# Two first-layer heads of a hybrid decoder trunk: output rows turned by transposing transfers, and taken over before and behind the next head's scores

## The chip, the cores and the metric

The kernel runs on one core of a Trainium2 chip. The metric is the device time of one execution in microseconds. A run of the kernel before gives 984.02 us as the median of three (984.0 to 984.71). The engines are TensorE (PE in the profile; its weight loads PEld), VectorE (DVE), ScalarE (ACT), GpSimd (POOL) and SyncE (SP), which issues most transfers; ScalarE issues some too.

## The reference

528 tokens (16 learned ones and 512 of input) of 1024 channels go through two layers, a gated linear attention with four heads of 512 output channels, and a differential softmax attention with eight; then comes a norm. The change lies in the first layer:

```python
proj = xn @ w_in
q, k, v, z, g_lr = jnp.split(proj, ...)
...
_, o_real = lax.scan(gla_chunk, S1, (chunks(q), chunks(k), chunks(v), chunks(lg)))
...
o = head_rms(o.transpose(0, 2, 1, 3)).reshape(B, L, D_INNER) * gnorm
y = jax.nn.silu(z) * o
return y @ w_out
```

`head_rms` normalizes the 512 channels of a token in one head. All of it is computed in float32.

## The kernel before

**Number format.** A float32 operand of TensorE is held as two rounded halves, hi and lo (`split`: a copy on ScalarE that makes hi, then a subtraction on VectorE that makes lo), and a product is three passes, hi*hi, hi*lo, lo*hi. So every weight tile gives a row such as wh<-raw on ScalarE and one such as wl<-raw on VectorE before TensorE can use it. Most projections are done in a scheme with sums of weight blocks (rows wl<-sum, a11h, a12h and the like), whose results land in the PSUM tiles bx, by, bv and are put together on ScalarE and VectorE as t, u, ks and so on.

**Layouts.** Projections come out with channels on partitions and tokens along the row. The state products of a head come out the other way, tokens on partitions. The output product needs channels on partitions again, so the outputs have to be turned.

**A head.** The loop over `hd` = 0 to 3 runs, for each head: the gate z; its scores (`gla_scores`, then `gla_cross` for blocks 1 to 4 through `gla_ready`); then `gla_blocks` over five blocks of tokens (block 0 has the 16 learned tokens, blocks 1 to 4 have 128 each). For a block, `output(b)` makes the products in a PSUM tile `po`, squares and sums them on ScalarE, takes the root on GpSimd, and scales `po` on ScalarE into the tile `on`, whose tag is t. `rows(b)` turns `on` by four TensorE transposes into a PSUM tile (L1258), multiplies by z on VectorE (L1260) and splits the product into y (L269 on ScalarE, L270 on VectorE). The output product of head `hd`, `q_gla_out`, reads y in the next head's iteration: for heads 0 and 1 behind the next head's v units, for head 2 among the blocks of head 3.

**The order of work on TensorE.** It is written by hand. A `Weaver` W holds a queue of generators of projection work. `W.fill(us)` takes from this queue for so many microseconds of estimated TensorE time, and is called between the steps of a head, so that TensorE has projections to do while the other engines finish a step. During the blocks of head `hd` the filling is the q and k units of head `hd`+1. `W.follow(...)` starts steps after so much woven TensorE time; a function put on `W.behind` runs right after the next weight load is issued; `W.land()` forces what is left of both; `W.finish()` empties the queue. The order on VectorE and ScalarE follows this program order, as scheduled when the kernel is built; instructions named `urgent` go ahead.

**Transposing transfers that are there already.** The first layer's v projections of later heads are not turned on TensorE but in memory (`turn_by_dma`): ScalarE copies a tile into two planes of 16-bit halves (L579), writes them to the DRAM tile vd (L580, on ScalarE's queue), and SyncE reads them back transposed into `b_all`, whose tag is keep (L588), and into lands (L590). What landed is split into hi and lo.

**Buffers.** PSUM has a ring of tiles named ps, used by transposes and products, and the banks bx, by, bv of the projections. Weight tiles raw come in by SyncE (L291, L278). The conditional loads kd<-steep and t<-steep (L1164, L1179) stand in SyncE's order within each head's scores; they move data only on a rare branch.

**Other lines the prediction names.** L421: matmuls of the projections. L390: the three-pass products in `output` and elsewhere. L1236: the scaling that makes `on`. L1195: products of the cross scores; L397, L398 and L400: their three-part split into cm; L1199: scaling of kd; c is the split of the larger cross scores. L852 and L853: the transposes of v that TensorE still does for head 3's v units. L467: the sum that ends the k projection.

Of the kernel before, what the change touches and what calls it, by code (L numbers as in the profile page):

```python
# [14 lines left out]
U16 = mybir.dt.uint16  # L15
# [5 lines left out]
P = 128  # L21
# [52 lines left out]
class Weaver:  # L74
# [15 lines left out]
    def defer(self, us, fn):  # L90
        self.late.append([us, fn])

    def follow(self, *steps):

        self.away.append([steps[0][0], list(steps)])

    def onward(self, us=0.0):
        for d in list(self.away):
            d[0] -= us
            while d[0] <= 0:  # L100
                d[1].pop(0)[1]()
                if not d[1]:
                    self.away.remove(d)
                    break
                d[0] += d[1][0][0]

    def land(self):

        while self.away or self.behind:
            self.onward(1000.0)  # L110
            while self.behind:
                self.behind.pop(0)()

    def spent(self, us):
        self.onward(us)
# [93 lines left out]
def trunk(ctx, tc, x, meta, g_norm, gla_w_in, gla_w_gate_up, gla_b_gate, gla_gnorm, gla_w_out,  # L209
# [21 lines left out]
    def T(p, shape, dt, tag, **kw):  # L231
        uid[0] += 1
        return p.tile(shape, dt, tag=tag, name=f"{tag}_{uid[0]}", **kw)
# [71 lines left out]
    def load(key):  # L305
        t = load_w(*key) if len(key) == 4 else load_blocks(*key)
        while behind:
            behind.pop(0)()
        return t

    def w_pair(shape):
# [256 lines left out]
    def turn_by_dma(planes, groups, ends, us, done, last):  # L568

        n = planes.shape[2]  # L570
        vd = T(dp, [2, P, 2, n], U16, "vd", bufs=3)
        rows = vd.rearrange("m p h c -> (m p h) c")
        raw = planes.rearrange("p m c -> p (m c)")[:, :2 * NR].rearrange("p (b c) -> p b c", c=2 * P)
        left, lands = [0, 1], []

        @urgent
        def leave(m, src):
            pl = words(planes[:, m, :]).rearrange("p (h c) -> p h c", h=2)
            act.activation(pl, words(src).rearrange("p (c h) -> p h c", h=2), AF.Copy)  # L579
            act.dma_start(vd[m], pl)  # L580
            left.remove(m)
            if not left:
                W.follow((4.0, lambda: behind.append(turn)))

        def turn():
            for blocks, c0 in groups:
                o = words(raw[:, blocks, :])
                tc.keep_in_program_order(sp.dma_start(o, rows[:, c0:c0 + P * o.shape[1]], transpose=True))  # L588
            lands.append(T(mp, [P, 1, 2 * P], F32, "lands"))
            tc.keep_in_program_order(sp.dma_start(words(lands[0]), rows[:, ends:ends + P], transpose=True))  # L590
            W.follow((us, place), (1.5, lambda: done(raw[:, :, :P], tick[0], 0)), (2.5, lambda: done(raw[:, :, P:], tick[0], 1)),
                     (1.5, rest))

        tick = []

        def rest():
            with tc.issue_after(W.split.ins):
                last(lands[0][:32, 0, :])

        def place():  # L600
            tick.append(T(mp, [P, 1], F32, "tick", bufs=2))
            tc.add_manual_dep(dve.memset(tick[0], 1.0).ins, W.mark.ins.name, mybir.DependencyInfo(
                mybir.DependencyClass.NoSync, mybir.DependencyReason.DATA), reason="place")

        return leave
# [338 lines left out]
    def q_gla_out(hd, s, sink=None):  # L944
        for i in range(2):
            ws.want_in_order((g_w_out, 512 * hd, 4, 512 * i), halves_of(256))

        def gen():
            turns[0] = 0
            for c in range(4):  # L950
                h = ws.take()
                for mm in range(2):
                    m = 2 * c + mm
                    banks = pb_pair()
                    for n, (k, q, p) in enumerate(PASSES):
                        for i in range(2):
                            pe.matmul(banks[i][:, :HT], h.t[p][:, k, mm * P:(mm + 1) * P], s.y[q][k][:, i * HT:(i + 1) * HT],  # L957
                                      start=n == 0, stop=n == len(PASSES) - 1)
                        if n % 3 == 2:
                            yield 0.68  # L960
                    if mm:
                        ws.done(h)
                    for i in range(2):
                        hh = hT[:, m, i * HT:(i + 1) * HT]
                        W.mark = dve.tensor_tensor(hh, hh, banks[i][:, :HT], op=ALU.add)
                    if sink is not None:
                        sink(m)
        return W.add(gen())
# [241 lines left out]
            gla_cross(hd, s, b)  # L1210
            W.fill(1.5)

    def gla_blocks(hd, s, fill, last):

        s.y = None

# [3 lines left out]
        @urgent  # L1220
        def output(b):
            t0, n = BLK[b]
            po = ps_tile()
            if b == 0:
                pe.matmul(po[:NM], s.am, s.vm, start=True, stop=True)
            else:
                mm3(po, [t[:, t0 - NM:t0 - NM + P] for t in s.a], val(b), True, False)
                for j in range(1, b):
                    c0 = ((b - 1) * (b - 2) // 2 + j - 1) * P
                    mm3(po, [t[:, c0:c0 + P] for t in s.c], val(j), False, False)  # L1230
                pe.matmul(po, s.cm[:, (b - 1) * P:b * P], s.vm, start=False, stop=True)
            on = tmp()[:, :512]
            st = T(tp, [P, 2], F32, "st")
            act.activation(on[:n], po[:n], AF.Square, accum_out=st[:n, 0:1])
            rstd_of(st[:n, 1:2], st[:n, 0:1], G_HV, n)
            act.activation(on[:n], po[:n], AF.Copy, scale=st[:n, 1:2])  # L1236
            return on

        def take_y():

# [10 lines left out]
        @urgent  # L1251
        def rows(b, on):
            t0, n = BLK[b]
            if b == 0:
                s.y, s.groups = take_y()
            pt = ps_tile()
            for m in range(4):
                pe.transpose(pt[:, m * n:(m + 1) * n], on[:n, m * P:(m + 1) * P], ident[:n, :n])  # L1258
            y = tmp()[:, :512].rearrange("p (m c) -> p m c", m=4)
            dve.tensor_tensor(y[:, :, :n], pt[:, :4 * n].rearrange("p (m c) -> p m c", m=4),  # L1260
                              s.z[:, :, t0:t0 + n], op=ALU.mult)
            for m0, m1, hi, lo in s.groups:
                split(hi[:, :, t0:t0 + n], lo[:, :, t0:t0 + n], y[:, m0:m1, :n])

        prev = None
        for b in range(5):
            W.fill(fill[0] if b else 0.6)
            if prev is not None:
                rows(b - 1, prev)
            prev = output(b)  # L1270
            W.fill(fill[1])
        W.fill(2.0)
        rows(4, prev)

    W.fill(5.0)
    pf = ps_tile()
# [15 lines left out]
    for hd in range(G_HEADS):  # L1292
# [30 lines left out]
        else:  # L1323
            W.stop = q_gla_v(hd + 1, heads[hd + 1])
        W.land()
        gla_blocks(hd, s, (1.2, 1.2) if last else (1.9, 1.6), last)
        W.finish()
        W.stop = None

# [573 lines left out]
```

## Time and profile before

| what | value |
|---|---|
| median of three runs | 984.02 us |
| lowest, highest | 984.0, 984.71 us |
| profiled execution | 984.03 us |
| its span on the core | 982.3 us |
| mean granted TensorE clock | 0.999 |
| bytes moved | 96.27 MB, 98 GB/s |

The span runs from the first to the last recorded instruction; what the execution takes beyond it, 1.7 us, lies outside the trace. Rows of the trace give the start and length of instructions in microseconds from the start of the span, the engine, the line, the operation with the tile written and the tiles read, the shapes, the number of equal instructions put into one row (xN), and in brackets an idle time ahead of it and what ended it. A row of a wait says which engine's instruction waited for which, with the total in microseconds, the number of waits and the longest. The shares of busy time in a stretch are in microseconds with the number of instructions behind.

### The profile page before, as it was taken

To read this page: it belongs to the slowest core of one execution; us is meant where nothing else is said; L and a number is where in the kernel's file an instruction comes from. 1 tells how busy PE (TensorE), PEld (TensorE's weight loads), DVE (VectorE), ACT (ScalarE), POOL (GpSimd) and SP (SyncE) were. 2 spreads that over 40 slices of the span, in tenths; PEclk is the share of its full clock that TensorE was granted. 3 is DMA by queue.
4 is the path that set the end of the run, shared out by engine and by line. 5 is a ranking of instruction groups with operands and counts; after the bars stand their busy time and mean duration, and the time that the engine had idled before them with its cause. 6 is when DMAs were issued, how large, how long until landed. Compare 5 with 4: busy or idle time off the path is not lost. (4 is left out here: it accounts for less than half of the span.)

```text
span 982.3 us, 18166 instructions
## 1 busy us (share of the span) xinstructions
PE 967.6 (99%) x7065; PEld 914.7 (93%) x7065; DVE 777.2 (79%) x1584; ACT 616.2 (63%) x1306; POOL 50.8 (5%) x68
## 2 busy tenths in 40 slices
PE   9999999999999999999999999999999999999997
PEld 8999999998999999999999998898998999989896
DVE  7899985887778787556998885977968879677785
ACT  7775755575546566536657675566764667655573
POOL 1000000000000000000001001001010000000001
PEclk9999999999999999999999999999999999999999
DMA  7322224621362222122322514234252251612212
GB/s 194 87 86 67 69 81 134 143 87 43 109 162 87 86 87 86 45 85 87 97 87 79 155 63 139 75 98 136 86 147 86 87 146 46 187 56 86 86 65 86
DMA packets 108490, 96.27 MB, mean 98 GB/s; under 512 B 33117, under 2 KB 94845, under 8 KB 108400
## 3 DMA queue, kind: packets, MB, share of 16 engines
q1 hardware_dynamic: 105520, 89.61, 30.7%
q10 hardware_dynamic: 2880, 5.46, 1.6%
q8 instruction: 57, 0.93, 0.4%
q14 instruction: 33, 0.27, 0.1%
HBM read 83.64 MB, written 7.57 MB: 93 GB/s over the span
## 5 line engine op out<-in xcount | busy, mean ns | idle before, releaser
L270 DVE TENSOR_TENSOR wl<-raw,wh 128x1024 fp32r<-128x1024 f32 x98 | 119.5, 1221 | 26.2 <-ACT wh L269 17.9
L269 ACT ACTIVATE wh<-raw 128x1024 fp32r<-128x1024 f32 x98 | 103.1, 1054 | 54.1 <-PE by L957 26.5
L421 PE MATMUL bv<-x,wh 128*128 128x264 f32 (+1 forms) x656 | 97.6, 287 | 0.6 <-DVE z L469 0.6
L421 PE MATMUL bx<-x,wh 128*128 128x264 f32 (+1 forms) x640 | 95.2, 286 | 0.5 <-ACT u L442 0.3
L421 PEld LDWEIGHTS bv<-x,wh 128*128 128x128 f32 x656 | 86.3, 189 | 1.2 <-DVE z L469 0.8
L421 PEld LDWEIGHTS bx<-x,wh 128*128 128x128 f32 x640 | 84.5, 188 | 1.7 <-ACT u L442 0.9
L270 DVE TENSOR_TENSOR wl<-sum,wh 128x1024 fp32r<-128x1024 f32 x41 | 50.1, 1222 | 17.6 <-ACT wh L269 15.7
L442 ACT ACTIVATE u<-bx 128x264 f32<-128x264 f32 (+1 forms) x120 | 45.4, 379 | 28.3 <-PE bx L421 24.9
L411 PE MATMUL bx<-x,wh 128*128 128x512 f32 (+1 forms) x256 | 62.5, 386 | 0.0
L1673 POOL TENSOR_TENSOR st<-st,mhalf 128x1 f32<-128x1 f32 x32 | 31.6, 987 | 465.4 <-ACT on L1671 447.2
L421 PE MATMUL bv<-x,wl 128*128 128x264 f32 (+1 forms) x328 | 55.2, 285 | 0.1
L421 PE MATMUL bx<-x,wl 128*128 128x264 f32 (+1 forms) x320 | 53.9, 285 | 0.0
L1637 ACT ACTIVATE p<-p,st 128x528 f32<-128x528 f32 (+3 forms) x64 | 36.4, 569 | 24.8 <-DVE st L1635 24.3
L411 PEld LDWEIGHTS bx<-x,wh 128*128 128x128 f32 x256 | 44.5, 188 | 7.9
L269 ACT ACTIVATE wh<-sum 128x1024 fp32r<-128x1024 f32 x41 | 43.2, 1054 | 12.3 <-PE bv L421 4.1
L421 PE MATMUL by<-x,a12h 128*128 128x264 f32 (+1 forms) x320 | 46.5, 285 | 0.0
L421 PE MATMUL bx<-x,a11h 128*128 128x264 f32 (+1 forms) x320 | 46.5, 285 | 0.0
L421 PEld LDWEIGHTS bv<-x,wl 128*128 128x128 f32 x328 | 45.9, 188 | 0.4 <-issue 0.3
L421 PEld LDWEIGHTS bx<-x,wl 128*128 128x128 f32 x320 | 45.0, 188 | 0.6 <-DVE wl L270 0.5
L269 ACT ACTIVATE a11h<-raw 128x512 fp32r<-128x512 f32 x41 | 25.8, 628 | 31.1 <-DMA raw<-in_diff_w_in_dram 15.8
L421 PEld LDWEIGHTS bx<-x,a11h 128*128 128x128 f32 x320 | 42.3, 188 | 0.8
L421 PEld LDWEIGHTS by<-x,a12h 128*128 128x128 f32 x320 | 41.7, 188 | 0.0
(479 smaller groups left out, 2639.4 us busy)
## 6 DMA issues: line engine op xcount, KB each, us to landing
raw<-in_gla_w_in_dram SPq DMA_DIRECT2D x48, 512.0 KB, 3.9
raw<-in_diff_w_in_dram SPq DMA_DIRECT2D x42, 512.0 KB, 4.6
raw<-in_diff_w_in_dram SPq DMA_DIRECT2D x11, 1024.0 KB, 5.7
raw<-in_gla_w_out_dram SPq DMA_DIRECT2D x8, 1024.0 KB, 5.2
raw<-in_diff_w_out_dram SPq DMA_DIRECT2D x8, 1024.0 KB
vd<-planes ACTq DMA_DIRECT2D x12, 268.0 KB, 3.0
vd<-keep ACTq DMA_DIRECT2D x8, 264.0 KB, 2.3
T<-bdr SPq DMA_DIRECT2D x8, 264.0 KB, 3.6
```

The lines of the kernel that those rows point to most:

```text
L269: act.activation(hi, src, AF.Copy)
L270: dve.tensor_tensor(lo, src, hi.bitcast(F32), op=ALU.subtract)
L411: pe.matmul(bank, a[:, k, :], b[k] if n0 is None else b[k][:, n0 + i * nn:n0 + (i + 1) * nn], start=n == 0 and ks[0] == 0, stop=n == len(t ...
L421: pe.matmul(bank[:, :x[q].shape[2]], w[p][:, k * P:(k + 1) * P], x[q][:, k, :], start=first and i == 0, stop=i == len(PASSES) - 1, skip_gr ...
L442: W.moved = act.activation(t, self.bx[:, :self.n], AF.Copy, scale=self.sc)
L1637: act.activation(p[:, :nk], p[:, :nk], AF.Exp, scale=-1.0, bias=st[:, m:m + 1], accum_out=st[:, 2 + m:3 + m])
L1673: pool.tensor_tensor(ms, ms, mhalf[:, :1], op=ALU.pow)
```

## The change

In heads 1 and 2 (`far`) the outputs of blocks 1 to 4 are no longer turned on TensorE. Blocks are taken in pairs, 1 with 2 and 3 with 4. After a block's scaling ScalarE copies `on` into two planes of 16-bit halves and writes them to a new DRAM tile yd (two writes a pair, 256 KB each). Four microseconds of woven TensorE time after the second write's place, one transposing transfer on SyncE reads the pair into half of `b_all` (keep). After 6.0 us more of woven time for the first pair, and 16.5 us for the second, VectorE multiplies the first block by z in place and ScalarE and VectorE split it into y; the second block follows 1.5 us later. So the first pair is taken over while the blocks still run, the second during the next head's scores. Block 0 is turned as before, and head 0 and head 3 turn all blocks on TensorE. `follow` and `land` get a tag, so that the output product can force the rows of its own head before it starts (`W.land(s)`).

The filling between blocks changes: heads 1 and 2 have 0.6 ahead of and 1.2 behind each block from 2 on (1.9 and 1.6 before), all heads 1.9 ahead of block 1 and 1.6 behind block 0.

```diff
+    def follow(self, *steps, tag=None):
+        self.away.append([steps[0][0], list(steps), tag])
+    def onward(self, us=0.0, tag=None):
+        for d in [d for d in self.away if tag in (None, d[2])]:
...
+    def land(self, tag=None):
+        while any(tag in (None, d[-1]) for d in self.away + self.behind):
+            self.onward(1000.0, tag)
...
         def gen():
             turns[0] = 0
+            W.land(s)
...
-    def gla_blocks(hd, s, fill, last):
+    def gla_blocks(hd, s, fill, last, far):
...
+        def far_rows(pair):
+
+            yd = T(dp, [2, P, 2, 512], U16, "yd", bufs=2)
+            src = yd.rearrange("m p h c -> (m p h) c")
+            i = pair[0] - 1
+            raw = b_all[:, i:i + 2, :].rearrange("p m c -> p (m c)")[:, :8 * P].rearrange("p (m c) -> p m c", m=4)
+            left = [0, 1]
+
+            @urgent
+            def leave(j, on):
+                pl = words(tmp()[:, :512]).rearrange("p (h c) -> p h c", h=2)
+                act.activation(pl, words(on).rearrange("p (c h) -> p h c", h=2), AF.Copy)
+                act.dma_start(yd[j], pl)
+                left.remove(j)
+                if not left:
+                    W.follow((4.0, turn), tag=s)
+
+            def turn():
+                tc.keep_in_program_order(sp.dma_start(words(raw), src, transpose=True))
+                W.follow((6.0 if i == 0 else 16.5, lambda: scaled_rows(0)), (1.5, lambda: scaled_rows(1)), tag=s)
+
+            def scaled_rows(j):
+                t0, n = BLK[pair[j]]
+                y = raw[:, :, j * P:(j + 1) * P]
+                with tc.issue_after(W.mark.ins):
+                    dve.tensor_tensor(y, y, s.z[:, :, t0:t0 + n], op=ALU.mult)
+                    for m0, m1, hi, lo in s.groups:
+                        split(hi[:, :, t0:t0 + n], lo[:, :, t0:t0 + n], y[:, m0:m1, :])
+
+            return leave
...
-        prev = None
+        prev, leave = None, None
         for b in range(5):
-            W.fill(fill[0] if b else 0.6)
-            if prev is not None:
+            W.fill(0.6 if b == 0 else 1.9 if b == 1 else fill[0])
+            if prev is not None and (b == 1 or not far):
                 rows(b - 1, prev)
             prev = output(b)
-            W.fill(fill[1])
-        W.fill(2.0)
-        rows(4, prev)
+            if far and b:
+                if b % 2:
+                    leave = far_rows((b, b + 1))
+                leave(1 - b % 2, prev)
+            W.fill(fill[1] if b else 1.6)
+        if not far:
+            W.fill(2.0)
+            rows(4, prev)
...
-        gla_blocks(hd, s, (1.2, 1.2) if last else (1.9, 1.6), last)
+        far = hd in (1, 2)
+        gla_blocks(hd, s, (1.2, 1.2) if last else (0.6, 1.2) if far else (1.9, 1.6), last, far)
```

Lines of the code behind the change stand one to three further on: L1258 becomes L1291, L421 becomes L422, L269 becomes L270.

**TensorE, head 1, between the outputs of blocks 2 and 3.** vm and cm are the operands of the learned tokens' share, v and a those of a block's own; x is the layer's input, the other names are weights. Before:

```order
L1231 MATMUL ps_5677<-vm_884_4660,cm_4864 128x512
L421 MATMUL bv_5582<-x_3_79,wh_5519 128x264 x8
L421 MATMUL bv_5582<-x_3_79,wl_5520 128x264 x4
L421 MATMUL bx_5640<-x_5_81,wh_5595 128x264 x8
L421 MATMUL bx_5640<-x_5_81,wl_5596 128x264 x4
L421 MATMUL by_5745<-x_2_78,a12h_5599 128x264 x8
L421 MATMUL by_5745<-x_2_78,a12l_5600 128x264
L1258 MATMUL ps_5755<-ident,t_5685 128x128 x4
L390 MATMUL ps_5764<-v_885_4661,a_905_4759 128x512
```

With the change:

```order
L1233 MATMUL ps_5654<-vm_884_4660,cm_4864 128x512
L422 MATMUL bx_5644<-x_1_77,a11l_5528 128x264 x3
L422 MATMUL by_5676<-x_6_82,a22h_5523 128x264 x8
L422 MATMUL by_5676<-x_6_82,a22l_5524 128x264 x4
L422 MATMUL bv_5582<-x_3_79,wh_5519 128x264 x3
L391 MATMUL ps_5696<-v_885_4661,a_905_4759 128x512
```

The four transposes of t are gone. Before, 33 projection matmuls stood between the two outputs; now it is 18, and the others have moved behind the outputs.

**ScalarE, head 2's cross scores.** cm and c are the parts of the cross scores, wh the hi halves of weights, keep the planes of head 3's v tiles, vd their DRAM tile, y the output rows of head 1. Before:

```order
L269 ACTIVATE wh_6072<-raw_5716 128x1024
L580 DMA vd_5540<-keep_83 128x1056
L579 ACTIVATE keep_83<-t_5959 128x1056
L397 ACTIVATE cm_6088<-ps_6091 32x128
L580 DMA vd_5540<-keep_83 128x1056
L398 ACTIVATE cm_6088<-ps_6091 32x128
L442 ACTIVATE u_6108<-bx_6028 128x264
L397 ACTIVATE cm_6088<-ps_6117 32x128
L398 ACTIVATE cm_6088<-ps_6117 32x128
L269 ACTIVATE wh_6135<-raw_5954 128x1024
L269 ACTIVATE c_1127_6089<-ps_6117 128x128
```

With the change:

```order
L580 ACTIVATE keep_83<-t_5945 128x1056
L399 ACTIVATE cm_6074<-ps_6077 32x128
L581 DMA vd_5540<-keep_83 128x1056
L443 ACTIVATE u_6094<-bx_6014 128x264
L398 ACTIVATE cm_6074<-ps_6103 32x128
L399 ACTIVATE cm_6074<-ps_6103 32x128
L270 ACTIVATE wh_6058<-raw_5735 128x1024
L270 ACTIVATE c_1125_6075<-ps_6103 128x128
L270 ACTIVATE wh_6121<-raw_5940 128x1024
L270 ACTIVATE y_1038_5606<-keep_83 128x4x128
```

The first of the two wh<-raw, ahead of all cm copies before, now stands behind both cross scores' copies, and the row y<-keep of head 1's second pair has come in behind the next wh<-raw.

**VectorE, head 3's scores.** kd and cm are parts of the cross scores, a11l and sum pieces of weights, v the lo half of values, c the lo half of cross scores. Before:

```order
L1199 TENSOR_SCALAR kd_7263<-kd_7263,eL_1012 128x16 x2
L400 TENSOR_TENSOR cm_7368<-ps_7371,cm_7368 32x128
L270 TENSOR_TENSOR wl_7346<-raw_6990,wh_7345 128x1024
L356 TENSOR_TENSOR raw_7228<-raw_7228 128x4x128
L270 TENSOR_TENSOR v_1309_7233<-ps_7388,v_1308_7232 128x4x128
L1199 TENSOR_SCALAR kd_7263<-kd_7263,eL_1012 128x144 x2
L402 SCALAR_TENSOR_TENSOR vm_1307_7231<-ps_7389,short,vm_1307_7231 32x128
L400 TENSOR_TENSOR cm_7368<-ps_7409,cm_7368 32x128
L469 TENSOR_TENSOR t_7439<-by_7402,u_7316 128x264
L270 TENSOR_TENSOR c_1338_7370<-ps_7409,c_1337_7369 128x128
```

With the change:

```order
L1201 TENSOR_SCALAR kd_7241<-kd_7241,eL_1012 128x16 x2
L401 TENSOR_TENSOR cm_7346<-ps_7349,cm_7346 32x128
L271 TENSOR_TENSOR wl_7324<-raw_7001,wh_7323 128x1024
L271 TENSOR_TENSOR a11l_7335<-raw_7206,a11h_7334 128x512
L357 TENSOR_TENSOR sum_7338<-raw_7206 128x512
L1201 TENSOR_SCALAR kd_7241<-kd_7241,eL_1012 128x144 x2
L357 TENSOR_TENSOR sum_7338<-sum_7338,raw_7206 128x512
L401 TENSOR_TENSOR cm_7346<-ps_7387,cm_7346 32x128
L470 TENSOR_TENSOR t_7417<-by_7380,u_7294 128x264
L357 TENSOR_TENSOR raw_7206<-raw_7206 128x4x128
L271 TENSOR_TENSOR c_1334_7348<-ps_7387,c_1333_7347 128x128
L271 TENSOR_TENSOR v_1305_7211<-ps_7366,v_1304_7210 128x4x128
```

The subtraction that makes c has come to stand behind a11l and the additions for sum, and v behind it; before, v stood ahead of c.

More of the change, by code (lines that the diff above doesn't have):

```diff
@@ L105, in onward @@
                 d[0] += d[1][0][0]
[L107 to L112, printed above, removed]
+    def land(self, tag=None):
+        while any(tag in (None, d[-1]) for d in self.away + self.behind):
+            self.onward(1000.0, tag)
+            for d in [d for d in self.behind if tag in (None, d[-1])]:
+                self.behind.remove(d)
+                d[0]()
     def spent(self, us):
@@ L307, in load @@
         while behind:
-            behind.pop(0)()
+            behind.pop(0)[0]()
         return t
@@ L582, in leave @@
             if not left:
-                W.follow((4.0, lambda: behind.append(turn)))
+                W.follow((4.0, lambda: behind.append((turn, None))))
         def turn():
```

4 lines of the change are left out of this document (removed).

## The prediction

> **What bounds the kernel now.** I read the page first, then the stretches around the two heads that change, then what TensorE waits for, and last the rows of the work that moves.
>
> ```profile
> PE 967.6 (99%) x7065; PEld 914.7 (93%) x7065; DVE 777.2 (79%) x1584; ACT 616.2 (63%) x1306; POOL 50.8 (5%) x68
> ```
>
> ```profile
> core 0: us, PE busy (x) PEld busy (x) DVE busy (x) ACT busy (x) POOL busy (x), PEclk, DMA share, GB/s
> 203.00:250.00 47.00, 46.00 (x346) 43.78 (x346) 37.11 (x71) 29.69 (x56) 3.12 (x5) 1.00 0.22 68
> 250.00:270.00 20.00, 20.00 (x170) 20.00 (x170) 13.23 (x30) 11.38 (x25) 0.00 (x0) 1.00 0.39 134
> ...
> 352.00:375.00 23.00, 22.51 (x190) 22.26 (x189) 21.64 (x45) 13.11 (x33) 0.00 (x0) 1.00 0.29 92
> ```
>
> TensorE is busy for all but 14.7 us of the 982.3, at full granted clock, so the time falls only where work leaves TensorE or one of its few waits goes, and any new wait adds in full. 203 to 250 is the stretch of head 1's output blocks. 250 to 270 and 352 to 375 are those in which the scores of head 2 and of head 3 run; the change puts its late rows there. ScalarE has room everywhere. VectorE has it in the first two, but not in the third: 21.64 of 23 us are busy.
>
> ```profile
> PE ps L1258 <- ACT t L1236: 1.6, 4, 0.6
> ```
>
> ```profile
> 227.34 0.28 PE L421 MATMUL by<-x,a12l 128*128 128x264 f32 x1
> 227.98 0.66 PE L1258 MATMUL ps<-ident,t 128*128 128x128 f32 x4 [0.35 <-ACT t L1236]
> 228.39 0.94 PE L390 MATMUL ps<-v,a 128*128 128x512 f32 x3
> ...
> 241.50 0.65 PE L421 MATMUL bv<-x,wl 128*128 128x264 f32 x4
> 242.79 0.66 PE L1258 MATMUL ps<-ident,t 128*128 128x128 f32 x4 [0.65 <-ACT t L1236]
> 243.20 1.22 PE L421 MATMUL bx<-x,wh 128*128 128x264 f32 x8
> ```
>
> ```profile
> 325.10 0.61 PE L1258 MATMUL ps<-ident,t 128*128 128x128 f32 x4
> 325.46 0.95 PE L390 MATMUL ps<-v,a 128*128 128x512 f32 x3
> ...
> 344.59 0.65 PE L421 MATMUL bv<-x,wl 128*128 128x264 f32 x4
> 345.44 0.66 PE L1258 MATMUL ps<-ident,t 128*128 128x128 f32 x4 [0.20 <-ACT t L1236]
> ```
>
> The first is a wait (who waited for whom: total, times, longest), the others are TensorE's own rows. What counts is the distance from one start to the next. Four turns of a block take 0.41 us at 227.98 and 0.36 us at 325.10.
>
> **What it removes.** Heads 1 and 2 lose the turns of blocks 1 to 4, 32 matmuls in eight groups: 8 x 0.38 = 3.1 us. Of the four waits, three stand before removed groups. A 264-column matmul starts 0.12 us after the one before (eight in 0.98), so those groups could have started at 227.46, 241.98 and 345.07: 0.52, 0.81 and 0.37 us, together 1.7. (The fourth stands before block 0, which stays.) The projection's matmuls are as many as before and only stand later, behind the outputs. Gain: 4.8 us.
>
> ```profile
> L1258 PE MATMUL ps<-ident,t x80: 207/272/329, 111.1 to 421.6; 128*128 128x128 f32 x64, 16*128 16x16 f32 x16
> ```
>
> By the 0.272 us that one turn lasts, the 32 would give 8.7 us; but they overlap, so I take the starts and keep this for a rival. The Trainium skill prices a 128x128 turn at 0.39 us on TensorE against 1.31 us by the DMA crossbar, and advises TensorE where PSUM will do (VectorE: DVE Perf Modes, The three transpose paths). By its 0.39 us the removal would be 12.5 us; the rows here contradict that, as they show 0.1 each in a full queue.
>
> **What it adds beside TensorE.**
>
> ```profile
> L579 ACT ACTIVATE planes<-t x12: 1079/1082/1100, 532.9 to 842.4; 128x1072 uint16<-128x1072 uint16 x12
> ```
>
> ```profile
> vd<-keep ACTq DMA_DIRECT2D x8, 264.0 KB, 2.3
> ```
>
> ```profile
> L588 SPq DMA_TRANSPOSE keep<-vd x4: 4037/4258/4601, 169.1 to 284.5; - x4
> ```
>
> ```profile
> 191.57 40.04 SPq L291 DMA_DIRECT2D raw<-in_gla_w_in_dram  x8
> 248.05 0.09 SPq L1164 DMA_DIRECT2D kd<-steep  x1
> ...
> 271.93 0.97 SPq L291 DMA_DIRECT2D raw<-in_gla_w_in_dram  x2
> 273.01 4.60 SPq L588 DMA_TRANSPOSE keep<-vd  x1
> 277.66 1.25 SPq L590 DMA_TRANSPOSE lands<-vd  x1
> ```
>
> ScalarE: eight copies into two planes of 1024 half words, about 1.03 us each after the row of 1072, in stretches where it idles a third. Each follows its own block's scaling, so it delays what stands behind it by 1 us: the split of the next weights, wanted on TensorE 24 to 36 matmuls (3 to 4 us) later. Without that cover it would cost up to 8 us. Eight writes of 256 KB land about 2.3 us after issue.
>
> SP: two transfers a head of the size in the keep row, 4.3 us of issue each. In SP's order both stand behind the fourth raw load, whose wait in the first row ends at 231.6, and ahead of the conditional kd load, which came at 248.05. SP has 16.4 us there and needs 8.6, so no weight load is held up: the next one stands behind kd. The second turn waits for block 4's write, at about 238.5 (an estimate, from laying the outputs' rows end to end without the turns), and is issued by 243, when VectorE is still making kd.
>
> ```profile
> DMA  9938998799999999999999299999995769790030
> ```
>
> ```profile
> 236.91 0.43 DVE L467 SCALAR_TENSOR_TENSOR ks<-bv,u 128x264 f32<-128x264 f32 x1
> ```
>
> Landing: this row is the DMA share in slices of 0.2 us from 273 to 281, from the turn at 273.01 on. It ends near 280.4, with the smaller lands transfer last; four fifths of the two are done at about 279, 6 us after issue. So the first pair, turned at about 231, is there at 237. On VectorE its product with z stands right behind the add of ks with u, which ran at 236.91; the projection now comes some 1 us later there, as the outputs stand ahead of it. I take no stall. Behind that product VectorE has wl<-sum, which TensorE wants at about 241.3 and which takes 1.2 us, so 1.8 us of lateness are covered; beyond that each costs TensorE the same.
>
> VectorE and ScalarE do the same z products and splits as before, later: the second pair of each head falls into the next head's scores. There I see two new waits, both by a place in an order.
>
> ```profile
> 258.40 1.05 PE L1195 MATMUL ps<-qs,kd 128*128 128x128 f32 x8
> 259.21 0.49 PE L421 MATMUL bv<-x,wh 128*128 128x264 f32 x2
> 259.53 0.65 PE L421 MATMUL bv<-x,wl 128*128 128x264 f32 x4
> 260.01 1.14 PE L421 MATMUL bx<-x,wh 128*128 128x264 f32 x8
> ```
>
> ```profile
> 259.85 0.27 ACT L398 ACTIVATE cm<-ps 32x128 fp32r<-32x128 f32 x1
> 260.14 1.06 ACT L269 ACTIVATE wh<-raw 128x1024 fp32r<-128x1024 f32 x1
> ```
>
> First, head 2's scores. The wh<-raw that the last product bx needs now stands behind the two cm copies of the second cross scores, where the split of output weights stood before. By those rows wh is done 1.99 us after the cross scores end on TensorE (261.20 against 259.21), while TensorE comes to it after six matmuls, 0.80 us (260.01): 1.2 us of wait. wl follows wh by another 1.2 us on VectorE with eight matmuls (0.98) as cover: 0.3 more. Cost 1.5 us; bounds 0.5 (if ScalarE reaches the copies without backlog) and 2.0.
>
> ```profile
> 363.21 0.61 PE L852 MATMUL ps<-ident,t 128*128 128x128 f32 x4
> 364.31 0.28 PE L853 MATMUL ps<-ident,t 128*32 128x128 f32 x1 [0.49 <-DVE v L270]
> ```
>
> ```profile
> 361.12 0.36 DVE L1199 TENSOR_SCALAR kd<-kd,eL 128x16 f32<-128x16 f32 x2
> 361.51 0.28 DVE L400 TENSOR_TENSOR cm<-ps,cm 32x128 fp32r<-32x128 f32 x1
> 361.83 1.23 DVE L270 TENSOR_TENSOR wl<-raw,wh 128x1024 fp32r<-128x1024 f32 x1
> ...
> 365.73 0.28 DVE L270 TENSOR_TENSOR c<-ps,c 128x128 fp32r<-128x128 f32 x1
> ```
>
> Second, head 3's scores. The second turn of v at L853 waited 0.5 us for a buffer of ps that the v split released. Now it waits for the split of c, which on VectorE stands behind a11l and two sums, and on ScalarE behind the copy of the very turns just ahead. At the least that is copy 0.6, c 0.3 and its split 0.3, with hand-overs 1.4 us. At the most VectorE comes as late to kd as here, 2 us after the cross scores, and needs 5.2 us from there to c (the 365.73 of this row plus 0.3): 2.8 us. I take 1.6, near the lower end, since none of its three links hangs on VectorE's backlog; it replaces 0.5: cost 1.1 net, bounds 0.9 and 2.3.
>
> Head 3's own blocks get two more units of filling, 1.4 us, ahead of block 1, and so less behind block 4; the next product there comes some 7 us after the last turn, so I cost it at nothing.
>
> **Sum.** 4.8 - 1.5 - 1.1 = 2.2 us: the profiled execution, 982.3 us of span and 984.03 in all, becomes 981.8. The median of the runs, 984.02, is the same to 0.01, so the forecast stands for it.
>
> **Rivals.** *Neither new wait comes:* if ScalarE and VectorE, which in the stretch from 203 to 250 have 17 and 10 us of idle time, arrive early, both costs go to their lower bounds or to nothing: 984.0 - 4.8 = 979.2. Against it stands the place of both instructions in their orders. *Given back:* both waits at their upper bounds, 4.8 - 2.0 - 2.3 = 0.5: 983.5. The 21.64 of 23 us of VectorE speak for it, since four more operations of 0.68 us enter that stretch. *The first turn lands late:* the one mechanism that makes it slower. VectorE stands at the z product, and all adds and splits behind it wait. It decides from a landing 7.8 us after issue, 6 and the 1.8 of cover.
>
> ```profile
> raw<-in_gla_w_in_dram SPq DMA_DIRECT2D x48, 512.0 KB, 3.9
> ```
>
> Raw loads share the queue. Behind one of these 3.9 us and a third of a second the landing is at 11 us; then TensorE loses 3.2 us in each of the two heads, and 984.0 - 2.2 + 6.4 = 988.2. Against it stand the 6 us above, measured right behind the raw load at 271.93, and the order, in which the fourth load has long been issued. *The turns free their whole duration:* 8.7 + 1.7 - 1.5 - 1.1 = 7.8, 976.2; the starts speak against it. That the change does not do what it says I see no room for: its rows are in the orders.
>
> **How the numbers follow.** Forecast (980.9 to 982.5) 0.45; neither wait 0.17; given back (982.5 to 985) 0.24; late landing 0.11; whole duration 0.03. The range runs from 979.2 to 985.0: it leaves out the late landing and the whole duration. Runs can be told apart from 0.2%, 2.0 us: faster is below 982.05, slower above 986.0. Faster: three quarters of the forecast, 0.34, with 0.17 and 0.03: 0.54. Slower: the late landing and a little of what an unseen wait would add to the third case, 0.13. Same: the rest, 0.33.
>
> **What would show it.** Right: no turns from L1291 in head 1 and 2 but block 0's; no wait for the scaled rows there; head 2's score matmuls some 3 us earlier; a wait of about 1 us for wh<-raw near 258; one of 1 to 3 us at L854 near 360, for c; the keep transfer landing 6 us after issue. Wrong: TensorE waiting for wl<-sum or ks right behind the first pair, which is the late landing; or waits for y at the start of the output product, which would mean that the second pair comes too late.

## The result, and the profile after

The changed kernel takes 988.62 us (median of six runs, 988.09 to 990.19), the kernel before beside it 984.33. The ratio is 1.0045, with an interval of 1.0033 to 1.0058: slower by 4.3 us, where 2.2 us less were forecast. The profiled execution is the slowest of the six, 990.19 us with a span of 988.4.

The first view is the engines' busy time on the page of the changed kernel, then its list of TensorE's waits (who waited for whom: total, times, longest):

```profile
PE 965.6 (98%) x7033; PEld 912.0 (92%) x7033; DVE 776.9 (79%) x1584; ACT 625.7 (63%) x1314; POOL 50.5 (5%) x68
```

```profile
PE ps L854 <- DVE c L271: 3.0, 1, 3.0
...
PE ps L391 <- DVE aT L271: 1.7, 2, 1.0
PE bx L422 <- DVE wl L271: 1.6, 1, 1.6
...
PE bx L422 <- ACT wh L270: 1.0, 1, 1.0
...
PE bv L422 <- DVE t L470: 0.9, 1, 0.9
```

The 32 matmuls are gone (7065 to 7033), and so is the line for turns that wait for ScalarE. But TensorE was busy 967.6 us of 982.3 before, and now 965.6 of 988.4: its idle time grew from 14.7 to 22.8 us. Four of the five waits shown are new; aT is 1.0 longer.

Where the time goes is best read from single rows of TensorE that both kernels have: the start of such a row now, less its start before, is the delay up to there. The table has this delay in us at seven rows, each named by its start before; the second column is another profile of the same changed kernel, and the last that of a kernel with three edits, both from the experiments below.

| row before (us) | place | changed | changed, again | three edits |
|---|---|---|---|---|
| 94.90 | first cross scores, ahead of all that changed | 1.21 | 0.07 | -0.93 |
| 248.40 | head 1's blocks done, scores of head 2 begin | 0.35 | -1.40 | -4.14 |
| 261.11 | third cross scores of head 2 | 3.02 | 1.29 | -2.60 |
| 351.05 | head 2's blocks done, scores of head 3 begin | 0.45 | -1.26 | -5.17 |
| 368.70 | fourth cross scores of head 3 | 4.28 | 2.47 | -6.39 |
| 429.02 | head 3's output product | 4.11 | 2.19 | -5.52 |
| 942.38 | late in the second layer | 5.87 | 3.80 | -5.32 |

The first line is the start of the program, which differs by up to 2.2 us between the profiles here and has nothing to do with the change. Below it, the first profile gains 0.86 us in head 1's blocks and 2.57 in head 2's, loses 2.67 and 3.83 us in the two stretches of scores, and another 1.8 far behind, near 905 us.

Head 1's blocks first: SyncE's, VectorE's and TensorE's rows in the changed kernel's timeline (start, length, engine, line, operation, in brackets the idle time ahead and what ended it):

```profile
232.52 5.27 SPq L1259 DMA_TRANSPOSE keep<-yd  x1
...
242.06 0.69 DVE L1266 TENSOR_TENSOR keep<-keep,z 128x512 f32<-128x512 f32 x1 [4.03 <-DMA keep<-yd]
242.67 1.22 DVE L271 TENSOR_TENSOR wl<-sum,wh 128x1024 fp32r<-128x1024 f32 x1
...
243.94 0.76 PE L422 MATMUL bx<-x,wl 128*128 128x264 f32 x4 [1.57 <-DVE wl L271]
```

The first pair was turned at 232.5 and had landed at 242.0, 9.5 us later and not 6. VectorE stood at the product with z for 4 us; wl<-sum is right behind it, and TensorE waited 1.57 us for that. In the second profile the same three numbers are 9.4, 3.55 and 0.97.

Then head 3's scores, TensorE and VectorE in the timeline and the granted clock by stretches of 2 us (columns: length, TensorE's busy time with its instructions, clock, DMA share, GB/s):

```profile
363.66 0.60 PE L853 MATMUL ps<-ident,t 128*128 128x128 f32 x4
367.24 0.37 PE L854 MATMUL ps<-ident,t 128*32 128x128 f32 x1 [2.98 <-DVE c L271]
367.26 2.11 PE L422 MATMUL bv<-x,wh 128*128 128x264 f32 x8
369.17 0.42 PE L422 MATMUL bv<-x,wl 128*128 128x264 f32 x1
...
366.81 0.28 DVE L271 TENSOR_TENSOR c<-ps,c 128x128 fp32r<-128x128 f32 x1
```

```profile
core 0: us, PE busy (x), PEclk, DMA share, GB/s
362.00:364.00 2.00, 2.00 (x20) 1.00 0.00 0
364.00:366.00 2.00, 0.26 (x3) 1.00 0.73 173
366.00:368.00 2.00, 0.76 (x4) 0.71 0.99 348
368.00:370.00 2.00, 2.00 (x11) 0.50 0.01 4
370.00:372.00 2.00, 2.00 (x18) 0.93 0.04 8
372.00:374.00 2.00, 2.00 (x20) 1.00 0.00 0
```

The turn of v waits for c as foreseen, but for 2.98 us. And the wait is not all: behind it eight matmuls of the projection take 1.91 us (367.26 to 369.17) instead of the 0.98 they take at full clock. The granted clock fell to a half at 366.9 us, while TensorE stood still, and came back 3.4 us later. The delay grows by 3.83 us over this stretch; the wait is 2.49 us longer than the 0.49 of before, so the slow clock took the other 1.34.

### The profile page after: what moved, and what is told of

The parts are those of the page before. It is cut to its first block, busy times and chain, and to the rows that moved or that the text cites. A ratio compares the mean times of both kernels' runs of the same rounds, so it can differ in the third digit from the quotient of the medians.

```text
span 988.4 us, 18137 instructions
## 1 busy us (share of the span) xinstructions
PE 965.6 (98%) x7033; PEld 912.0 (92%) x7033; DVE 776.9 (79%) x1584; ACT 625.7 (63%) x1314; POOL 50.5 (5%) x68
## 5 line engine op out<-in xcount | busy, mean ns | idle before, releaser
L270 ACT ACTIVATE wh<-raw 128x1024 fp32r<-128x1024 f32 x98 | 103.1, 1054 | 54.4 <-PE by L959 26.6
L422 PE MATMUL bv<-x,wh 128*128 128x264 f32 (+1 forms) x656 | 99.1, 289 | 1.7 <-DVE t L470 0.9
L422 PE MATMUL bx<-x,wh 128*128 128x264 f32 (+1 forms) x640 | 95.2, 286 | 1.5 <-ACT wh L270 1.0
L422 PEld LDWEIGHTS bv<-x,wh 128*128 128x128 f32 x656 | 87.2, 190 | 2.8 <-DVE t L470 1.1
L422 PEld LDWEIGHTS bx<-x,wh 128*128 128x128 f32 x640 | 84.6, 188 | 2.9 <-ACT wh L270 1.6
L422 PE MATMUL bx<-x,wl 128*128 128x264 f32 (+1 forms) x320 | 54.4, 286 | 1.6 <-DVE wl L271 1.6
L422 PE MATMUL bv<-x,wl 128*128 128x264 f32 (+1 forms) x328 | 55.3, 285 | 0.1
L270 ACT ACTIVATE wh<-sum 128x1024 fp32r<-128x1024 f32 x41 | 43.3, 1055 | 15.5 <-DVE sum L357 4.7
L422 PEld LDWEIGHTS bx<-x,wl 128*128 128x128 f32 x320 | 45.3, 188 | 2.8 <-DVE wl L271 2.5
L422 PE MATMUL by<-x,a12h 128*128 128x264 f32 (+1 forms) x320 | 46.6, 285 | 0.2 <-DVE ks L468 0.2
L422 PEld LDWEIGHTS bv<-x,wl 128*128 128x128 f32 x328 | 46.0, 189 | 0.4 <-issue 0.3
L422 PE MATMUL bx<-x,a11h 128*128 128x264 f32 (+1 forms) x320 | 46.2, 285 | 0.0
L270 ACT ACTIVATE a11h<-raw 128x512 fp32r<-128x512 f32 x41 | 25.8, 628 | 31.7 <-DMA raw<-in_diff_w_in_dram 17.4
L422 PEld LDWEIGHTS bx<-x,a11h 128*128 128x128 f32 x320 | 42.1, 188 | 0.6
L422 PEld LDWEIGHTS by<-x,a12h 128*128 128x128 f32 x320 | 41.7, 188 | 0.4 <-DVE ks L468 0.4
```

Of the source, the lines that this page charges most:

```text
L270: act.activation(hi, src, AF.Copy)
L422: pe.matmul(bank[:, :x[q].shape[2]], w[p][:, k * P:(k + 1) * P], x[q][:, k, :], start=first and i == 0, stop=i == len(PASSES) - 1, skip_gr ...
```

## The experiments

All kernels are the changed one with the edit shown, measured beside the kernel before, which read 984.45 to 984.67 us in these sessions.

**The same kernel again.** No edit.

> The changed kernel once more, unaltered, so that a second profile of it stands beside the first. Theory A (the loss is three waits in the changed stretch, fixed by the order of work): 0.3 to 0.5% slower than before, with waits on TensorE of 1 to 2 us for wl in head 1, about 1 us for wh near 262 us, and 2.5 to 3.5 us for c near 367 us with a granted clock of about 0.5 right behind it. Rival B (that one profile was an unlucky execution): two of the three waits are gone or below 0.5 us, and the time is within 0.2% of before. The waits ahead of 100 us and near 910 us, together 2.8 us in the first profile, should differ by theory A as much between the two profiles of this kernel as between it and before.

It took 988.64 us, ratio 1.0039 (1.0024 to 1.0055). The waits are the same: 3.0 us for c with the clock at 0.50 behind it, 1.0 for wh, 1.0 for wl, 0.9 for t, 1.7 for aT. The start of the program was 1.1 us quicker. So rival B falls. The place near 905 us came out as slow as in the first profile, against what theory A says of it: that loss belongs to the kernel, too, and is taken up further down.

**One head at a time.**

```diff
-        far = hd in (1, 2)
+        far = hd == 1
```

> Only head 1 uses the transposing transfers; head 2 is turned on TensorE again. Theory A: gain in head 1 of 1.5 us of turns and 1.3 us of waits, loss of 1.7 us (wl), 0.9 us (t) and 1.3 us (wh and wl): slower than before by 1 us, 985.3; no wait over 1 us for c near 365 us and no fall of the clock there. Rival C (a common cause such as the changed filling or the second layer makes the loss): as slow as both heads together, 987 or more.

986.49 us, 1.0018 (1.0009 to 1.0026). From 94.90 to 429.02 this kernel neither gains nor loses (delay 0.06 and 0.00): 1.48 us are gained in head 1's blocks, 2.67 lost in the scores of head 2, and 1.25 won back behind them, in stretches where head 2 and head 3 work as before. The rest, 1.8 us, is lost in the second layer, 0.95 of it near 905 us. So on balance what this kernel loses does not lie in the heads; 985.3 were expected.

The same line with `hd == 2`:

> Only head 2 uses the transposing transfers; head 1 is turned on TensorE again. Theory A: gain 1.9 us, loss 2.5 us of wait for c and 1.3 us of slow clock: slower than before by 2 us, 986.2; the waits for wl and wh in head 1 and behind it are gone. Rival C: 987 or more. Rival D (the late landing carries the loss): no slower than before, since the first pair's landing in head 2 cost TensorE nothing in the first profile.

987.68 us, 1.0028 (1.0017 to 1.0039). Head 2's blocks gain 1.82 us, and head 3's scores lose 5.79: a wait of 3.3 us for c, then almost 6 us at half clock. Here are the stretches of this kernel with that wait, columns as above:

```profile
362.00:364.00 2.00, 0.67 (x6) 1.00 0.33 54
364.00:366.00 2.00, 0.03 (x2) 0.69 1.02 362
366.00:368.00 2.00, 2.00 (x10) 0.50 0.35 117
368.00:370.00 2.00, 2.00 (x11) 0.50 0.00 0
370.00:372.00 2.00, 2.00 (x13) 0.60 0.00 0
372.00:374.00 2.00, 2.00 (x19) 1.00 0.00 0
```

Head 2 alone is slower than before, so rival D falls. Rival C asked for 987 us or more of both; the first stays below, and the next kernel settles it. The two do not add up (1.9 and 3.1 us against 4.1 for both). The slow clock cost 2.99 us in this profile and 1.34 in that of both heads, which goes that way; but the profile is that of the slowest of seven runs, 1.6 us above their median, so how much of the difference this explains is not shown.

**Neither head.** `far = False`.

> No head uses the transposing transfers; what is left of the change is the filling of 1.9 ahead of block 1 and 1.6 behind block 0, which alters head 3 alone. Theory A: within 0.5 us of before. Rival C: slower by more than 1 us.

984.5 us, 0.9997 (0.9988 to 1.0005): the new filling costs nothing, as forecast.

**The first pair taken over later.**

```diff
-                W.follow((6.0 if i == 0 else 16.5, lambda: scaled_rows(0)), ...
+                W.follow((9.0 if i == 0 else 16.5, lambda: scaled_rows(0)), ...
```

> The first pair of each head is taken over 9.0 instead of 6.0 us of woven time behind its transposing transfer; all else as in the changed kernel. Theory A (the z product stands in VectorE's order before its data is there, and wl for head 1's projection stands behind it): VectorE's idle time ahead of the first product with z falls from 3.5 to 4 us to below 1, TensorE's wait for wl near 243 us (1.0 to 1.6) goes, and the wait for c near 365 us falls to about 1.6, since c stands 1.4 us further ahead in VectorE's order there: 1.5 to 4 us faster than the changed kernel. Rival E (other work on VectorE holds wl up, the landing only coincides): the wait for wl stays.

983.01 us, 0.9985 (0.9976 to 0.9993): 5.6 us below the changed kernel, where 1.5 to 4 were expected, and faster than before. The wait for wl is gone, and rival E with it. The wait for t, 0.9 us, is gone too, and the one for c is down to 1.06 us, with the clock at 1.00 throughout.

**The first transfer ahead of the fourth weight load.**

```diff
-                    W.follow((4.0, turn), tag=s)
+                    W.follow((1.0 if i == 0 else 4.0, turn), tag=s)
...
-                W.follow((6.0 if i == 0 else 16.5, lambda: scaled_rows(0)), ...
+                W.follow((9.0 if i == 0 else 16.5, lambda: scaled_rows(0)), ...
```

> The first pair's transposing transfer stands 3 us of woven time earlier, and so ahead of the fourth weight load of SyncE's order instead of behind it; its rows stay where they were in time. Theory F (the landing took 8 to 9.5 us because it ran beside a weight load issued just ahead): it lands 5 to 7 us after issue, and the wait for wl near 243 us goes, 1 to 1.6 us faster than the changed kernel. Rival G (the transfer takes so long by itself, or because of the write of block 4): it lands 8 us or more after issue here too; the weight load behind it is then late and TensorE waits for its halves.

983.21 us, 0.9989 (0.998 to 0.9998). SyncE's, VectorE's and TensorE's rows of this kernel in the timeline:

```profile
228.22 1.98 SPq L1259 DMA_TRANSPOSE keep<-yd  x1
230.31 1.12 SPq L292 DMA_DIRECT2D raw<-in_gla_w_in_dram  x2
...
236.70 0.68 DVE L1266 TENSOR_TENSOR keep<-keep,z 128x512 f32<-128x512 f32 x1
...
360.91 0.28 DVE L271 TENSOR_TENSOR c<-ps,c 128x128 fp32r<-128x128 f32 x1
361.34 0.27 PE L854 MATMUL ps<-ident,t 128*32 128x128 f32 x1 [1.72 <-DVE c L271]
```

VectorE no longer waits for the landing, in neither head. How early the data is there can be read from the trace: for every transfer it keeps sixteen semaphore updates that tell of its landing, and in the changed kernel VectorE's product starts right behind the last of them (9.52 us after issue, the product at 9.54). In this kernel the last one comes 4.44 us after issue in head 1 and 5.82 in head 2. Here is what the DMA moved in the changed kernel, from the issue at 232.52 on, and then in this one, from 228.22 on (columns: length, VectorE's busy time, clock, DMA share, GB/s):

```profile
232.50:237.00 4.50, 2.67 (x6) 1.00 0.90 279
237.00:238.50 1.50, 0.43 (x1) 1.00 2.43 237
238.50:239.50 1.00, 0.00 (x0) 1.00 0.21 6
239.50:240.80 1.30, 0.00 (x0) 1.00 0.99 254
```

```profile
228.20:229.50 1.30, 1.22 (x1) 1.00 0.00 0
229.50:232.30 2.80, 0.86 (x2) 1.00 1.14 234
232.30:237.30 5.00, 2.68 (x6) 1.00 0.84 289
```

By the size of their packets (256 bytes for the transposing transfer, 1 KB for the load), the first row of the changed kernel is the weight load and the write of one block, and the transposing transfer's data begin only at 236.9, 4.4 us after issue. Here they begin 1.3 us after issue and are through at 232.2, and the load follows. So the transfer was late because it stood behind the load: theory F's mechanism, with a landing even sooner than its 5 to 7 us in head 1, and rival G falls. No wait for the later load shows on TensorE.

The run also gives the price of the lateness, since in head 2 VectorE's order from the product with z to c is that of the changed kernel: the product comes without a wait in both heads, c's wait is 1.72 us instead of 2.98, and the clock stays at 1.00. The time is 5.4 us below the changed kernel where 1 to 1.6 were expected, as more than the wait for wl hung on the landing.

**Head 3's v turns later.**

```diff
         def turned_back(m, vt):
...
-            W.defer(2.4, post)
+            W.defer(5.4, post)
```

> The turns of head 3's v on TensorE are put 5.4 instead of 2.4 us behind their projection; all else as in the changed kernel. Theory A (the turn of v stands on TensorE ahead of the moment at which VectorE frees its buffer by the split of c): the wait of 3.0 us for c near 365 us falls below 0.5 and the granted clock stays at 1.0 behind it, since TensorE no longer stands still: 2.5 us of wait and 1.2 us of slow clock, 3.7 us faster than the changed kernel, 984.9. Rival H (VectorE is so full in that stretch that the wait only moves to another row): a wait of 2 us or more for VectorE stays in 352 to 380, and the time is less than 1.5 us below the changed kernel.

983.05 us, 0.9983 (0.9974 to 0.9992), 5.6 us below the changed kernel and more than expected. The wait for c is gone, but 1.4 us of wait for v's own split have come in its place, so rival H has half a point; the clock stays at 1.00. In this profile the landing cost only 0.3 us at wl, and nothing was lost near 905 us.

**All three edits.**

> The three edits together: the first pair's transfer ahead of the fourth weight load, its rows 3 us later, and head 3's v turns 3 us later. Theory A: both big waits are gone, 3.7 and 1.5 us below the changed kernel, 983.2 to 983.6, which is 1 us faster than before; the waits for t and wh near 260 us (0.9 and 1.0) stay and keep it from the 4.8 us that the removed turns are worth.

979.17 us, 0.9954 (0.994 to 0.9967): 5.5 us below before, 9.5 below the changed kernel, and better than expected. Of the waits for moved work the list of this kernel has left:

```profile
PE bx L422 <- ACT wh L270: 1.0, 1, 1.0
...
PE ps L854 <- DVE v L271: 0.4, 1, 0.4
```

**The last edit alone,** with `far = False`:

> No head uses the transposing transfers, and head 3's v turns are 3 us later: the control for the last edit. Theory A (that edit only takes away the wait for the buffer): it can win the 0.5 us that the turn of v waited in the kernel before, no more: 0 to 0.6 us faster than before. Rival I (the edit is worth more by itself, and the kernel with all three edits is fast because of it): 1.5 us or more faster than before.

984.54 us, 1.0 (0.9991 to 1.0009): it wins nothing by itself. The 5.5 us are the transfers' gain, once nothing takes it back.

**Three heads.** With all three edits and `far = hd < 3`:

> As the kernel with all three edits, with head 0 on the transposing transfers too, so that 16 more turns leave TensorE. Theory A (each head is worth its 1.5 us of turns and 0.4 to 1.3 us of waits for the scaled rows where its late rows meet no full engine): 1.5 to 2.5 us faster than the kernel with all three edits, 977. Rival J (in head 0 something new waits, as VectorE and ScalarE are busier in the first 200 us): no faster than that kernel.

983.62 us, 0.999 (0.9981 to 0.9999). In this kernel the landing of head 0's second pair overwrites decay sums in `b_all` that head 1 still needs, so head 1's values are not the reference's; the amount of work is the same. It is 4.5 us slower than with two heads, as rival J has it: at 203 us it is 4.0 us behind that kernel, with a new wait of 2.1 us for t, 3.4 us of half clock behind it, and a wait of 0.9 for ks.

**The second pair sooner.** With all three edits:

```diff
-                W.follow((9.0 if i == 0 else 16.5, lambda: scaled_rows(0)), ...
+                W.follow((9.0 if i == 0 else 12.0, lambda: scaled_rows(0)), ...
```

> As the kernel with all three edits, with the second pair taken over 12.0 instead of 16.5 us of woven time behind its transfer. In ScalarE's order a split of output rows (0.63 us) and the copy of c (0.26) come to stand ahead of the wh for which TensorE waits 1.0 us near 260 us. Theory A (that wait is set by wh's place in ScalarE's order): it grows to 1.7 to 2.0 us, and the time is 0.5 to 1.2 us above the kernel with all three edits, 980.0. Rival K (it is set by the weight load or by TensorE's own lead): it stays at 1.0 us within 0.2.

983.24 us, 0.9985 (0.9976 to 0.9993). First two rows of ScalarE and one of TensorE from this kernel's timeline, then the stretches with its other wait:

```profile
256.11 0.63 ACT L270 ACTIVATE y<-keep 128x512 fp32r<-128x512 f32 x1
...
256.80 1.05 ACT L270 ACTIVATE wh<-raw 128x1024 fp32r<-128x1024 f32 x1
...
257.90 1.24 PE L422 MATMUL bx<-x,wh 128*128 128x264 f32 x8 [1.67 <-ACT wh L270]
...
368.06 0.27 PE L854 MATMUL ps<-ident,t 128*32 128x128 f32 x1 [2.12 <-DVE v L271]
```

```profile
366.00:368.00 2.00, 0.00 (x0) 1.00 0.00 0
368.00:370.00 2.00, 1.94 (x10) 0.56 0.00 0
370.00:372.00 2.00, 2.00 (x13) 0.59 0.00 0
372.00:374.00 2.00, 2.00 (x19) 1.00 0.00 0
```

The wait for wh grew from 1.0 to 1.67 us, as much as the rows put ahead of it: ScalarE's order sets it, not the load, and rival K falls. The time rose by 4.1 us, more than that, since the v split on VectorE is late as well and 2.12 us of wait bring the slow clock again.

## Why the prediction was wrong

**What was removed: right.** Head 1's blocks gain 3.21 us and head 2's 2.57 in the kernel with three edits (-0.93 to -4.14, -2.60 to -5.17): 5.8 us where 4.8 were forecast. But the waits for scaled rows that went with the turns differ between profiles: in the three kernels whose head 1 is as before (head 2 alone, neither head, v later alone), the stretch of head 1's blocks is 0.52 to 1.02 us shorter than in the one profile of before, too. That leaves 4.8 to 5.3 us for the change.

**The landing: the step that failed.** "So the first pair, turned at about 231, is there at 237 ... I take no stall." The turn's own time in the order was nearly right, 232.5 and 231.0 in the two profiles; the 6 us were not. They came from a row of the DMA share in which two transfers lay one upon the other, and no row showed anyone taking over the data. The end of a busy stretch is not the landing: by the semaphore updates in the trace of before, the transfer issued at 273.01 had landed 7.41 us after issue. In the changed kernel the first pairs landed after 9.5 and 9.4 us in head 1, and 8.0 in head 2, past the 7.8 us that the rival of the late landing named as its point of decision. Its place in the queue made them late, right behind a weight load. The further 1.4 us of head 1 go with a pause: from 238.5 to 239.5 the transfer all but stops, during and right behind a 16 KB packet that the profile's page counts under `q8 instruction`. In all five profiles with head 1's first transfer behind the load such a packet runs before it has landed, and the landing takes 9.35 to 9.52 us; in the five with head 2's there, none does, and it takes 7.51 to 8.08.

That rival, with a chance of 0.11 and a forecast of 988.2, is what happened, in a wider form, and with the sign that the prediction named for it, TensorE waiting for wl<-sum behind the first pair. That its figure lies so near the 988.6 is luck: it charged TensorE 3.2 us in each of two heads, and the direct wait is 1.57 us for wl in head 1 alone. The rest of the price is VectorE's backlog. The wait for t, 0.9 us, goes when the landing is in time (first pair later, first transfer ahead). In head 2 VectorE stood still for 1.45 us; here are its row there, and its busy time from there to c, in the changed kernel (columns as for the DMA above):

```profile
344.52 0.69 DVE L1266 TENSOR_TENSOR keep<-keep,z 128x512 f32<-128x512 f32 x1 [1.45 <-DMA keep<-yd]
```

```profile
344.50:367.00 22.50, 22.26 (x44) 1.00 0.39 104
```

It has no idle time left in which to make that up, 22.26 of 22.50 us, and 22 us later c is late by it: 2.98 us of wait against 1.72 where the transfer went ahead.

**First new wait, wh and wl in head 2's scores: right.** 1.5 us were forecast. In the kernels without the wait for t, head 2's scores lose 1.55 and 1.54 us (-2.61 to -1.06 with the first pair later, -4.14 to -2.60 with three edits), of which wh is 1.0.

**Second new wait, c in head 3's scores: the right mechanism, the wrong size.** "I take 1.6, near the lower end, since none of its three links hangs on VectorE's backlog". They do: the upper end of the prediction, 2.8, was the better one, and 2.98 was measured. Where VectorE was not late it is 1.72, close to the 1.6.

**The slow clock: not in the sum at all.** The prediction took the clock as given: it stood at 1.00 in each of the three stretches it read. The Trainium skill has the rule (TensorE: Matmul & The Clock Gate, Part 1: The HAM clock gate): TensorE goes to half clock after an idle window of about 3.4 us, and back after as much work. The half agrees with the 0.50 here, and so does the time at it, 3.41 us in four profiles and 6.83 in that of head 2 alone. The idle time does not, as waits of 2.08, 2.12, 2.97, 2.98 and 3.29 us brought it, while 1.57, 1.67 and 1.72 did not.

**The filling and the extra work of ScalarE: right,** they cost nothing that shows (neither head: 984.5).

With the landing in time, the forecast comes near: 983.0 and 983.2 us against 981.8, faster than before by 1.7 and 1.5 us where 2.2 were said, and both still lose 1.1 to 1.3 us near 905.

**The 1.7 us near 905 us: not in the sum either.** There TensorE waits for aT because a weight load lands late; the load's issue and its first use, before and with the change:

```profile
895.49 0.92 SPq L291 DMA_DIRECT2D raw<-in_diff_w_in_dram  x2
...
900.88 0.69 DVE L356 TENSOR_TENSOR sum<-raw 128x512 f32<-128x512 f32 x1 [2.76 <-DMA raw<-in_diff_w_in_dram]
```

```profile
899.72 0.92 SPq L292 DMA_DIRECT2D raw<-in_diff_w_in_dram  x2
...
906.76 0.69 DVE L357 TENSOR_TENSOR sum<-raw 128x512 f32<-128x512 f32 x1 [4.42 <-DMA raw<-in_diff_w_in_dram]
```

5.4 us became 7.0. It is not the number of transfers: the kernels with v's turns later and with three edits issue as many, and lose nothing there. What differs is one packet. Here is the row that the DMA view of the changed kernel has for the 8 us from that issue, and that of before has not:

```profile
q8 instruction: 1, 0.02, 1.1%
```

It is again a packet of 16 KB, and it starts 2.54 us after the load's issue and takes 1.40. The thirteen profiles part by it. In six (the changed kernel twice, each head alone, first pair later, first transfer ahead) such a packet starts between 0.2 us ahead of the issue and 3.2 us behind it, and the load is first used 6.0 to 7.1 us after issue. In the other seven there is none, or only one from 4.4 us on, and the first use comes after 5.1 to 5.5 us. So the loss goes with where this packet falls, and a change hundreds of microseconds ahead moved it. This rests on timing alone: no run moved the packet by itself.

**The sum again.** From 94.90 to 942.38 the first profile loses 4.66 us. What the forecast left out makes that up: 1.57 for wl, 0.9 for t, 1.4 by which the net wait for c, 2.49, exceeds its 1.1, 1.34 of slow clock and 1.7 near 905 are 6.9, and less the 2.2 that were forecast they are 4.7.

## What to carry to other kernels

Work that leaves the bounding engine for a transfer is paid for where its result is taken over: an instruction on an in-order engine that stands in line before its data is there holds up everything behind it, and on an engine without idle time the loss is carried on until someone needs its last row, here 22 us later. Put the taking-over behind the latest landing that a consumer's wait has shown, not behind the end of a busy stretch of the DMA; three microseconds more of distance were worth 5.6 us here. And count a wait of the matmul engine of two to three microseconds twice, as the clock may fall to half behind it.

## What had not been expected of the hardware

The granted clock fell to 0.50 in all five profiles with a single wait of 2.08 us or more (up to 3.29), and behind no wait of up to 1.72. It stayed there for 3.41 us in four of them and 6.83 in one, which cost 1.3 to 3.0 us beyond the wait where this could be told apart. Why one was twice as long is open.

A transposing transfer's issue held SyncE for 5.27 us right behind a weight load and 1.98 us ahead of it, for the same bytes. Its landing took 7.5 to 9.5 us behind the load and 4.1 to 6.0 ahead of it; the second pairs of the changed kernel, with no load ahead, took 4.1 and 4.4.

In the late load near 905 us the transfers together are as fast as before until 5.4 us after issue, and then a thin stream goes on for 1.6 us. These are the DMA rows of the two kernels, in slices of 0.2 us from the load's issue:

```profile
GB/s 0 0 0 0 0 102 164 133 138 164 287 343 389 389 384 374 399 379 379 399 359 350 344 380 391 275 64 11 0 0 0 0 0 0 0 0 0 0 0 0
```

```profile
GB/s 0 0 0 0 0 123 143 118 128 215 297 343 435 353 374 359 348 374 369 358 359 382 371 416 332 184 73 47 20 26 26 20 32 21 21 11 0 0 0 0
```

20 to 30 GB/s is about a sixteenth of the 380 that all 16 engines move in the middle of the load. That fits one engine held up by the packet of 16 KB while the consumer waits for the last; the trace does not name the engine of a packet.
